# Turning attention probabilities by transposing transfers instead of identity matmuls

## The chip, the cores and the metric

The kernel runs on one core of one Trainium2 chip. The metric is the device time of one execution in microseconds (us), lower is better; the output must agree with the reference. An engine is named as the profile names it: PE is TensorE's matmul stream and PEld its weight loads, DVE is VectorE, ACT is ScalarE, POOL is GpSimd, SP is the engine whose queue issues most transfers.

## The reference

Two layers share a residual stream of 256 tokens by 2048 features, all in float32. The first uses differential attention, the second multi-head latent attention; each then cross-attends into 256 memory tokens and applies a squared-ReLU MLP.

```python
# differential attention, one block of 128 query rows
s = jnp.einsum('bqhcd,bkhcd->bhcqk', qi, k).astype(jnp.float32) * scale
s = jnp.where(causal_mask(q0, S), s, -jnp.inf)
p = jax.nn.softmax(s, axis=-1)
a = (p[:, :, 0] - lam * p[:, :, 1]).astype(v.dtype)
return jnp.einsum('bhqk,bkhd->bqhd', a, v)
...
# latent attention, one block of 128 query rows
s = jnp.einsum('bqhd,bkhd->bhqk', qi, k).astype(jnp.float32) * scale
s = jnp.where(causal_mask(q0, S), s, -jnp.inf)
p = jax.nn.softmax(s, axis=-1).astype(v.dtype)
return jnp.einsum('bhqk,bkhd->bqhd', p, v)
```

What matters here is the step between the two einsums. The softmax runs along a row, so the scores lie with queries on the partitions; the weighted sum over keys needs the probabilities with keys on the partitions. So each 128x128 block of probabilities has to be turned.

## The kernel before

**Arithmetic.** Every float32 factor of a matmul is split into a high part (a cast to PE's reduced float32, on ACT) and a low part (the difference, on DVE); a product is three matmuls: high by high, high by low, low by high. So every operand that is made on the way, the turned probabilities too, costs one ACT cast and one DVE subtract.

**Weights.** They stream from HBM in units of 128 x 2048 words (1 MB) into a pool of seven `raw` buffers (`RAWS`), are split in halves of 1024 columns into `whi` and `wlo` (L221, L222; four buffers each), and are used by PE for 24 matmuls of 512 columns. `take` hands out the next unit and `fill` loads and splits ahead, four units (`AHEAD`). All these loads are issued by SP (`load`, L189) and kept in program order.

**The order.** PE's order is written out by the program itself: the dense work (projections, MLP) runs in a line, and side work is put between by a small planner. A `Task` is a generator that yields a number of us, by a clock that counts PE's planned time, after which its next piece is emitted (`pump`). The constants are `T_SM` 6.5, `T_EV` 2.6, `T_TURN` 2.6, `T_LAND` 7.0 and others. The orders of ACT, DVE and POOL are made by a scheduler from the dependencies. Up to four PSUM banks serve side tasks (`side_bank`, `give_back`).

**Attention.** Both attentions run in four groups of heads. In group gi the attention is started (`attend`), then the projection of the group before it is multiplied (latent; the differential one weaves its projections in later), then the next group's queries, keys and values are made (`project`). So an attention's small steps lie between the dense matmuls of other groups.

- Differential (`attend_diff`): three blocks a group. Each makes scores in a PSUM bank, a softmax, and the difference `a` (128 x 256 words), waits `T_SM + 6.3 + slack`, turns `a` with two flips (`prob_T`), splits it into a `raw` buffer, waits `T_TURN + 1.6`, and multiplies by the values.
- Latent and cross (`attend4`): two head pairs p and two row tiles t give four blocks a group. Each makes scores, a softmax and the normalised `p` (128 x 256 words for t = 0 under the causal mask, else 128 x 512), waits `T_SM + slack`, turns it with two or four flips, and splits it into `pTs`, two `raw` buffers that the group holds until its weighted sum. The weighted sum (`weighted`) starts once all four blocks are done.

A flip (L174) is a matmul by the identity, which puts a turned 128x128 block into PSUM.

**Transposing transfers already in use.** Activations in other places are turned by the DMA rings: `half_words` copies a tile on ACT into two planes of 16-bit halves (low and high halves of each float32, L377), POOL stores them to DRAM (`turned`, L379), SP issues a transposing transfer back into SBUF (`turned_by_dma`, L384, 16-bit elements), and the landed halves lie so that they read as float32 again. 66 tiles take this way, in the projections of the differential attention and in the MLP.

**Buffers.** `p`, `planes`, `landed`, `xg`, `os`, `ks` and the rows and tiles of the rotary embedding all come from one ring of seven SBUF tiles of 128 x 512 words (tag `ev`, `EVS = 7`).

Of the kernel before, what the change touches and what calls it, by code (L numbers as in the profile page):

```python
# [10 lines left out]
F32 = mybir.dt.float32  # L11
F32R = mybir.dt.float32r
I32 = mybir.dt.int32
U16 = mybir.dt.uint16
# [4 lines left out]
P = 128  # L19
# [3 lines left out]
CH = 512  # L23
# [7 lines left out]
EVS = 7  # L31
# [21 lines left out]
def trunk(ctx, tc, x, xT, xT0, mem, memT, positions, gcols, gfinal, lam_vecs, consts, W, out):  # L53
    nc = tc.nc
# [9 lines left out]
    work = pool("work", 2)  # L64
# [6 lines left out]
    def nm(s):  # L71
        serial[0] += 1
        return f"{s}_{serial[0]}"
# [88 lines left out]
    def give_back():  # L162
        free_banks[0] += 1
# [8 lines left out]
    def flip(o, src):  # L172
        clock[0] += 0.109
        nc.tensor.transpose(o, src, ident)  # L174
# [207 lines left out]
    def turned_by_dma(there):  # L382
        landed = work.tile([P, 4, 2 * P], U16, tag="ev", name=nm("landed"), bufs=EVS)
        tc.keep_in_program_order(nc.sync.dma_start_transpose(landed, there))  # L384
        return landed.bitcast(F32).rearrange("p k t -> p k t")

    def split_landed(dst, t, src):
        at = slice(t * P, (t + 1) * P)
        hi = dst[:, 0, :, at]
        tc.keep_in_program_order(nc.scalar.copy(hi, src))  # L390
        nc.vector.tensor_tensor(dst[:, 1, :, at], src, f32(hi), ALU.subtract)  # L391
# [234 lines left out]

    def prob_T(src, n, pt):

        for i in range(n):
            flip(pt[:, i * P : (i + 1) * P], src[:, i * P : (i + 1) * P])  # L630
        o = raw_tile().bitcast(F32R)[:, : 2 * CH].rearrange("p (a c) -> p a c", a=2)
        nc.scalar.copy(o[:, 0, : n * P], pt[:, : n * P])
        nc.vector.tensor_tensor(o[:, 1, : n * P], pt[:, : n * P], f32(o[:, 0, : n * P]), ALU.subtract)
        return o
# [21 lines left out]
    def masks(n):  # L656
        return mask.unsqueeze(1).broadcast_to([P, n, P])

    def attend4(score_pairs, inputs, v, dst, causal, scales=(1.0, 1.0), slack=0.0):


        pTs = [raw_tile().bitcast(F32R).rearrange("p (a b c d) -> p a b c d", a=2, b=2, c=2) for _ in range(2)]

        def probs(t, p, nk):


            sb = yield from side_bank()
            heads = (2 * p, 2 * p + 1)
            pr = work.tile([P, CH], F32, tag="ev", name=nm("p"), bufs=EVS)[:, : 2 * nk]
            rows = pr.rearrange("p (h k) -> p h k", k=nk)  # L670
            if nk == P:
                view = sb.rearrange("p (h a k) -> p h a k", h=2, a=2)
                scores(view, [score_pairs(h, True) for h in heads], t, False)
                nc.vector.tensor_tensor(rows, view[:, :, 1], masks(2), ALU.add)
                nc.vector.tensor_tensor(rows, rows, view[:, :, 0], ALU.add)
                pr, rs = softmax(pr, 2, pr, scales[t])
            else:
                scores(sb.rearrange("p (h k) -> p h k", k=nk), [score_pairs(h, False) for h in heads], t, causal)
                pr, rs = softmax(sb, 2, pr, scales[t])
            nc.vector.tensor_tensor(rows, rows, rs[:, :2].unsqueeze(2).broadcast_to([P, 2, nk]), ALU.mult)  # L680
            yield T_SM + slack
            nb = nk // P
            for i in range(2 * nb):
                flip(sb[:, i * P : (i + 1) * P], pr[:, i * P : (i + 1) * P])
            src = sb[:, : 2 * nk].rearrange("p (h b q) -> p h b q", h=2, b=nb)
            hi = pTs[p][:, 0, :, :nb, t * P : (t + 1) * P]
            nc.scalar.copy(hi, src)
            nc.vector.tensor_tensor(pTs[p][:, 1, :, :nb, t * P : (t + 1) * P], src, f32(hi), ALU.subtract)
            give_back()
            yield T_TURN  # L690

        def weighted(po, p, i, kb, passes, first, last):
            vt = v() if callable(v) else v
            q = slice(kb * P if causal else 0, S)
            o = po[:, i * S : (i + 1) * S][:, q]
            for j, (sv, sp) in enumerate(passes):
                mmul(
                    o, val(vt, sv, kb, (2 * p + i) * P, P), pTs[p][:, sp, i, kb, q],
                    first and j == 0, last and j == len(passes) - 1,
                )  # L700

        def result(p, po):
            hi = dst[:, 0, 2 * p : 2 * p + 2, :]
            src = po.rearrange("p (h q) -> p h q", h=2)
            with urgent():
                nc.scalar.copy(hi, src)
                nc.vector.tensor_tensor(dst[:, 1, 2 * p : 2 * p + 2, :], src, f32(hi), ALU.subtract)

        PASSES = ((0, 0), (0, 1), (1, 0))

        def task():
            for i in inputs:
                yield i
            blocks = []
            for p in range(2):
                for t in range(NT):
                    blocks.append(Task(probs(t, p, P if causal and t == 0 else S)))
                    yield 1.3
            for b in blocks:
                yield b  # L720
            if causal:
                for p in range(2):
                    po = yield from side_bank()
                    for i in range(2):
                        for kb in range(2):
                            weighted(po, p, i, kb, PASSES, kb == 0, kb == 1)
                    result(p, po)
                    give_back()
                    yield 1.3
            else:  # L730
                pos_ = []
                for p in range(2):
                    pos_.append((yield from side_bank()))
                while not v():
                    yield 0.5
                for p in range(2):
                    for i in range(2):
                        weighted(pos_[p], p, i, 0, PASSES, i == 0, False)
                for p in range(2):
                    for passes in (PASSES[:2], PASSES[2:]):  # L740
                        for i in range(2):
                            weighted(pos_[p], p, i, 1, passes, False, passes == PASSES[2:] and i == 1)
                    result(p, pos_[p])
                    give_back()
            yield T_TURN

        dst.run(task())

    def attend_diff(q, k, v, dst, coef, subcols, slack=0.0):


        def block(t, heads, out):
            nk = (t + 1) * P
            sb = yield from side_bank()
            comps = [s for h in heads for s in (2 * h, 2 * h + 1)]
            scores(sb.rearrange("p (c k) -> p c k", k=nk), [whole(q, k, s, nk) for s in comps], t, True)
            n = 2 * len(heads)
            with urgent():
                pr, rs = softmax(sb, n)
                nc.vector.tensor_tensor(rs[:, :n], rs[:, :n], coef[:, :n], ALU.mult)  # L760
                a = work.tile([P, S], F32, tag="a", name=nm("a"))
                for i in range(len(heads)):
                    p0 = pr[:, 2 * i * nk : (2 * i + 1) * nk]
                    p1 = pr[:, (2 * i + 1) * nk : (2 * i + 2) * nk]
                    ai = a[:, i * nk : (i + 1) * nk]
                    nc.vector.tensor_scalar(ai, p1, rs[:, 2 * i + 1 : 2 * i + 2], None, ALU.mult)
                    nc.vector.scalar_tensor_tensor(ai, p0, rs[:, 2 * i : 2 * i + 1], ai, ALU.mult, ALU.add)
            yield T_SM + 6.3 + slack
            pT = prob_T(a, 2, sb)
            give_back()  # L770
            yield T_TURN + 1.6
            if not out:
                out.append((yield from side_bank()))
            po = out[0]
            nb = nk // P
            for i, h in enumerate(heads):
                for kb in range(nb):
                    blk = slice((i * nb + kb) * P, (i * nb + kb + 1) * P)
                    mm3(
                        po[:, h * S : (h + 1) * S], pT[:, 0, blk], pT[:, 1, blk],  # L780
                        val(v, 0, kb, h * S, S), val(v, 1, kb, h * S, S), kb == 0, kb == nb - 1,
                    )
# [792 lines left out]
    def project_diff(gi):  # L1575
# [14 lines left out]
    da_slacks = [0.0, 0.0, 2.0, 1.2]  # L1590
    norm, m, mk = attention(
        project_diff,
        lambda h, o: attend_diff(*h, o, coef, gsub, da_slacks.pop(0)),
        lambda gi: mem_norm() if gi == 1 else None,
        G_CROSS, da_pairs,
    )
# [150 lines left out]
    def attend_latent(held, o):  # L1747
        qr, q, k, v = held
        attend4(
            lambda h, first: side_by_side(q, k, h) + [(qr[:, h], (krope[:, :, :P],))]  # L1750
            if first
            else whole(q, k, h, S) + [(qr[:, h], (krope[:, 0], krope[:, 1]))],
            qr.tasks + q.tasks + k.tasks + krope.tasks, v, o, True, rq, slacks.pop(0),
        )

    norm, m, mk = attention(project_latent, attend_latent, sooner, G_CROSS + 16)
# [150 lines left out]
```

## Time and profile before

| | |
|---|---|
| median of three runs | 2170.72 us |
| range of the runs | 2170.44 to 2171.89 us |
| span of the profiled execution, first to last instruction (the profile has no other time for it) | 2169.0 us |
| granted PE clock, mean | 0.999 |
| differential attention with its projections | about 0 to 390 us |
| latent attention with its projections | about 1150 to 1410 us |
| matmuls of PE, recorded | 10187 |
| moved by the DMA rings | 543.89 MB, mean 251 GB/s |

How it is read: busy time of an engine is the union of its instructions' durations. PE's matmuls are pipelined, so their durations overlap and the distance between starts is what one costs. A list of waits names, for an engine and line, what ended an idle time before it, with the total, the number of times and the longest. A row of a group gives line, engine, operation, out<-in, shapes and count, and then shortest, median and longest duration in ns or the busy time and mean. A `q` after an engine means its sequencer or its queue.

### The profile page before, as it was taken

How to read it: one execution, taken by the hardware profiler on the slowest of the kernel's cores; microseconds unless marked ns; L12 is line 12 of the kernel's file. 1: busy time of each engine (PE TensorE's matmuls, PEld its weight loads, DVE VectorE, ACT ScalarE, POOL GpSimd, SP SyncE). 2: the span in 40 equal slices, each digit the busy share in tenths (PEclk: the TensorE clock that was granted, in tenths of full speed). 3: DMA queues.
4: the chain of work that ended last, by engine and by line, in shares of the span. 5: the costliest groups of instructions: out<-in, count | busy, mean ns of one | idle time of the engine just before them, and what ended most of it. 6: DMA issues, size and time to landing. Idle time of an engine off the chain costs nothing.

```text
span 2169.0 us, 27519 instructions
## 1 busy us (share of the span) xinstructions
PE 2155.4 (99%) x10187; PEld 1805.5 (83%) x10187; DVE 1740.2 (80%) x1962; ACT 1465.6 (68%) x1938; POOL 221.0 (10%) x336
## 2 busy tenths in 40 slices
PE   9999999999999999999999999999999999999998
PEld 7888888888888888888889988888888888888887
DVE  6656878788788889788886878778888888888887
ACT  7556756666767777776665755666777778677665
POOL 1113210001000000000000420000000000000001
PEclk9999999999999999999999999999999999999999
DMA  9477896548989999998986344645998999999895
GB/s 386 151 248 234 260 293 222 194 151 267 297 280 267 308 282 256 319 274 260 306 251 218 103 170 155 221 168 182 283 299 292 258 317 280 266 285 310 254 315 149
DMA packets 151863, 543.89 MB, mean 251 GB/s; under 512 B 79536, under 2 KB 79920, under 8 KB 92848
## 3 DMA queue, kind: packets, MB, share of 16 engines
q1 hardware_dynamic: 134496, 440.14, 56.9%
q0 software_dynamic: 16800, 101.20, 22.5%
q8 instruction: 80, 1.31, 0.2%
q10 hardware_dynamic: 432, 0.79, 0.1%
q14 instruction: 55, 0.45, 0.1%
HBM read 505.38 MB, written 19.40 MB: 242 GB/s over the span
## 4 chain that ended last, share of the span: by engine, by line
PE 95%; DVE 3%; DMA 1%; issue 1%; ACT 0%; DVEq 0%; POOLq 0%; POOL 0%
PE mm L170 62%; PE pr L170 28%; PE ax L170 3%; DVE wlo L222 1%; DMA raw<-in_mlp_wup_dram 1%; PE ax L174 1%; PE mm L174 1%; DVE raw L887 0%; DVE unit L391 0%; ACT whi L221 0%; DVE x L545 0%; DMA raw<-in_da_wqkv_dram 0%; PE pr L174 0%; DVE p L680 0%; DVE ev L1722 0%
## 5 line engine op out<-in xcount | busy, mean ns | idle before, releaser
L222 DVE TENSOR_TENSOR wlo<-raw,whi 128x1024 fp32r<-128x1024 f32 (+3 forms) x946 | 1138.8, 1217 | 335.5 <-ACT whi L221 313.7
L221 ACT CAST whi<-raw 128x1024 fp32r<-128x1024 f32 (+2 forms) x945 | 985.3, 1045 | 576.8 <-PE mm L170 420.0
L170 PE MATMUL mm<-whi,unit 128*128 128x512 f32 (+2 forms) x4000 | 1271.2, 389 | 1.3 <-DVE unit L391 0.9
L170 PEld LDWEIGHTS mm<-whi,unit 128*128 128x128 f32 x4000 | 749.1, 188 | 149.6 <-DVE unit L391 1.7
L170 PE MATMUL mm<-wlo,unit 128*128 128x512 f32 (+2 forms) x2000 | 774.1, 387 | 0.2
L170 PE MATMUL pr<-whi,unit 128*128 128x512 f32 x1912 | 610.5, 389 | 0.0
L170 PEld LDWEIGHTS mm<-wlo,unit 128*128 128x128 f32 x2000 | 376.2, 188 | 72.8 <-DVE wlo L222 3.0
L170 PEld LDWEIGHTS pr<-whi,unit 128*128 128x128 f32 x1912 | 358.8, 188 | 73.4
L170 PE MATMUL pr<-wlo,unit 128*128 128x512 f32 x956 | 372.3, 389 | 1.5 <-DVE wlo L222 1.5
L170 PEld LDWEIGHTS pr<-wlo,unit 128*128 128x128 f32 x956 | 179.7, 188 | 40.0 <-DVE wlo L222 3.6
L379 POOL DMA_DIRECT2D turned<-planes x66 | 37.7, 572 | 673.5 <-ACT planes L377 661.2
L887 DVE TENSOR_TENSOR raw<-raw,raw 128x2048 f32<-128x2048 f32 x40 | 91.5, 2288 | 8.8 <-DMA raw<-in_mlp_wup_dram 8.6
L545 DVE TENSOR_TENSOR x<-x,mm 128x512 f32<-128x512 f32 x128 | 85.3, 682 | 14.1 <-PE mm L170 14.0
L879 POOL DMA_DIRECT2D raw<-in_mlp_wup_dram x48 | 43.4, 905 | 447.8 <-DVE wlo L222 445.2
L431 POOL TENSOR_TENSOR rs<-rs,mhalf 128x1 f32<-128x1 f32 (+1 forms) x26 | 24.9, 962 | 408.1 <-DVE rs L430 408.0
L222 DVE TENSOR_TENSOR wlo<-unit,whi 128x1024 fp32r<-128x1024 f32 x48 | 57.3, 1221 | 5.2 <-ACT whi L221 4.0
L221 ACT CAST whi<-unit 128x1024 fp32r<-128x1024 f32 x48 | 49.8, 1053 | 9.7 <-PE pr L170 9.7
L377 ACT COPY planes<-p 128x1024 uint16<-128x1024 uint16 x48 | 50.0, 1041 | 0.3
L170 PE MATMUL mm<-unit,whi 128*128 128x256 f32 x256 | 46.9, 285 | 0.0
L425 ACT ACTIVATE junk<-x 128x512 bf16<-128x512 f32 (+1 forms) x57 | 35.3, 620 | 10.1 <-DVE x L1092 5.0
L1457 ACT ACTIVATE p<-p,r 128x512 f32<-128x512 f32 x42 | 30.4, 724 | 16.4 <-DVE p L962 7.4
L170 PEld LDWEIGHTS mm<-unit,whi 128*128 128x128 f32 x256 | 40.2, 192 | 0.3
(199 smaller groups left out, 1280.7 us busy)
## 6 DMA issues: line engine op xcount, KB each, us to landing
raw<-in_mlp_wdown_dram SPq DMA_DIRECT2D x128, 1024.0 KB, 7.3
raw<-in_mlp_wup_dram SPq DMA_DIRECT2D x120, 1024.0 KB, 6.9
raw<-in_mlp_wup_dram POOLq DMA_DIRECT2D x48, 1024.0 KB, 9.1
raw<-in_da_wqkv_dram SPq DMA_DIRECT2D x45, 1024.0 KB, 9.8
turned<-planes POOLq DMA_DIRECT2D x66, 256.0 KB, 6.4
raw<-in_da_wo_dram SPq DMA_DIRECT2D x16, 1024.0 KB, 7.0
raw<-in_ca_wkv_dram SPq DMA_DIRECT2D x16, 1024.0 KB, 6.7
raw<-in_mlp_wdown_dram POOLq DMA_DIRECT2D x16, 1024.0 KB, 10.7
```

The source lines that it names most:

```text
L170: return nc.tensor.matmul(o, stationary, moving, start=start, stop=stop, skip_group_check=onto)
L174: nc.tensor.transpose(o, src, ident)
L221: nc.scalar.copy(hi, r)
L222: nc.vector.tensor_tensor(lo, r, f32(hi), ALU.subtract)
L377: nc.scalar.copy(planes, src.bitcast(U16).rearrange("p (w s) -> p s w", s=2))
L379: nc.gpsimd.dma_start(there.rearrange("(q s) w -> q s w", s=2), planes)
L425: return nc.scalar.activation(junk[:, : src.shape[1]], src, AF.Square, scale=scale, accum_out=acc)
L431: nc.gpsimd.tensor_tensor(r[:, :n], r[:, :n], mhalf.broadcast_to([P, n]), ALU.pow)
L545: nc.vector.tensor_tensor(xc, xc, ps, ALU.add)
L879: tc.keep_in_program_order(nc.gpsimd.dma_start(onto, src, accum_op=ALU.add))
L887: nc.vector.tensor_tensor(o, o, q, ALU.add)
L1457: nc.scalar.activation(r, src, AF.Relu, scale=rstd[t])
```

## The change

In the differential attention's groups 0 to 2 and the latent attention's groups 1 to 3 (`sent`), the flips are replaced. ACT copies the probabilities into two 16-bit planes in SBUF (`planes_of`); SP issues one transposing transfer that reads the planes from SBUF and writes the turned planes to SBUF (`turned_planes`), with no store to DRAM and no POOL work; ACT joins the two landed planes into float32 words (`words_of`). The split into high and low part then reads these words from SBUF in place of PSUM. The PSUM bank of the scores is given back before the transfer is issued, and the planner's waits become `T_SM`, `T_EV`, `T_LAND`, `T_TURN + 1.0` in the latent attention, and the old wait, `T_LAND`, `T_TURN + 1.6` in the differential one. The three new tiles of a block come from the `ev` ring. The other groups and the cross attention stay as they were.

```diff
+    def planes_of(src):
+        n = src.shape[1]
+        planes = work.tile([P, 2 * n], U16, tag="ev", name=nm("planes"), padded_shape=[P, 2 * CH], bufs=EVS)
+        nc.scalar.copy(planes.rearrange("p (s w) -> p s w", s=2), src.bitcast(U16).rearrange("p (w s) -> p s w", s=2))
+        return planes
+
+    def turned_planes(planes):
+        n = planes.shape[1] // P
+        landed = work.tile([P, n * P], U16, tag="ev", name=nm("landed"), padded_shape=[P, 2 * CH], bufs=EVS).rearrange("p (n t) -> p n t", t=P)
+        tc.keep_in_program_order(nc.sync.dma_start_transpose(landed, planes))
+        return landed
+
+    def words_of(landed):
+        n = landed.shape[1] // 2
+        words = work.tile([P, n * P], F32, tag="ev", name=nm("words"), padded_shape=[P, CH], bufs=EVS).rearrange("p (n t) -> p n t", t=P)
+        nc.scalar.copy(words.bitcast(U16).rearrange("p k (t s) -> p s k t", s=2), landed.rearrange("p (s k) t -> p s k t", s=2))
+        return words
...
     def prob_T(src, n, pt):
 
-        for i in range(n):
-            flip(pt[:, i * P : (i + 1) * P], src[:, i * P : (i + 1) * P])
+        if pt is not None:
+            for i in range(n):
+                flip(pt[:, i * P : (i + 1) * P], src[:, i * P : (i + 1) * P])
+        else:
+            pt = src.rearrange("p k t -> p (k t)")
...
-            yield T_SM + slack
             nb = nk // P
-            for i in range(2 * nb):
-                flip(sb[:, i * P : (i + 1) * P], pr[:, i * P : (i + 1) * P])
-            src = sb[:, : 2 * nk].rearrange("p (h b q) -> p h b q", h=2, b=nb)
+            if sent:
+                planes = planes_of(pr)
+                yield T_SM
+                give_back()
+                yield T_EV
+                landed = turned_planes(planes)
+                yield T_LAND
+                src = words_of(landed).rearrange("p (h b) q -> p h b q", h=2)
+            else:
+                yield T_SM + slack
+                for i in range(2 * nb):
+                    flip(sb[:, i * P : (i + 1) * P], pr[:, i * P : (i + 1) * P])
+                src = sb[:, : 2 * nk].rearrange("p (h b q) -> p h b q", h=2, b=nb)
...
-            give_back()
-            yield T_TURN
+            if not sent:
+                give_back()
+            yield T_TURN + (1.0 if sent else 0.0)
...
+                planes = planes_of(a) if sent else None
             yield T_SM + 6.3 + slack
-            pT = prob_T(a, 2, sb)
-            give_back()
+            if sent:
+                give_back()
+                landed = turned_planes(planes)
+                yield T_LAND
+                pT = prob_T(words_of(landed), 2, None)
+            else:
+                pT = prob_T(a, 2, sb)
+                give_back()
             yield T_TURN + 1.6
...
-        lambda h, o: attend_diff(*h, o, coef, gsub, da_slacks.pop(0)),
+        lambda h, o: attend_diff(*h, o, coef, gsub, da_slacks.pop(0), bool(da_slacks)),
...
-            qr.tasks + q.tasks + k.tasks + krope.tasks, v, o, True, rq, slacks.pop(0),
+            qr.tasks + q.tasks + k.tasks + krope.tasks, v, o, True, rq, slacks.pop(0), len(slacks) < 3,
```

More of the change, by code (lines that the diff above doesn't have):

```diff
@@ L657, in masks, with attend4 @@
         return mask.unsqueeze(1).broadcast_to([P, n, P])
-    def attend4(score_pairs, inputs, v, dst, causal, scales=(1.0, 1.0), slack=0.0):
+    def attend4(score_pairs, inputs, v, dst, causal, scales=(1.0, 1.0), slack=0.0, sent=False):
         pTs = [raw_tile().bitcast(F32R).rearrange("p (a b c d) -> p a b c d", a=2, b=2, c=2) for _ in range(2)]
@@ L747, in attend4, with attend_diff @@
         dst.run(task())
-    def attend_diff(q, k, v, dst, coef, subcols, slack=0.0):
+    def attend_diff(q, k, v, dst, coef, subcols, slack=0.0, sent=False):
         def block(t, heads, out):
```

## The prediction, made before the changed kernel was run

> **What bounds the kernel now.** I read the page first, then PE's waits, then PE's timeline around the transposes by identity.
>
> ```profile
> span 2169.0 us, 27519 instructions
> PE 2155.4 (99%) x10187; PEld 1805.5 (83%) x10187; DVE 1740.2 (80%) x1962; ACT 1465.6 (68%) x1938; POOL 221.0 (10%) x336
> PE 95%; DVE 3%; DMA 1%; issue 1%; ACT 0%; DVEq 0%; POOLq 0%; POOL 0%
> ...
> PE pr L170 <- DVE wlo L222: 1.5, 3, 1.1
> ...
> PE mm L170 <- DVE unit L391: 0.9, 2, 0.5
> PE ax L174 <- DVE ev L1722: 0.7, 2, 0.5
> ```
>
> The chain that ended last is PE for 95% of the span, and PE's list of waits holds only a few us in all. So PE's instruction stream is the time: what leaves it is saved, and every new wait in it is paid in full. One of the few waits (0.7 us in two places) is at a transpose in the latent attention, where rotary rows are late.
>
> What a removed transpose is worth is read from starts, since a matmul's own duration overlaps its neighbour's:
>
> ```profile
> 1314.77 0.39 PE L170 MATMUL mm<-whi,unit 128*128 128x512 f32 x1
> 1315.01 0.60 PE L174 MATMUL ax<-identr,p 128*128 128x128 f32 x4
> 1315.36 0.47 PE L170 MATMUL mm<-whi,unit 128*128 128x512 f32 x1
> 1315.67 0.40 PE L170 MATMUL mm<-wlo,unit 128*128 128x512 f32 x1
> 1315.91 0.63 PE L170 MATMUL mm<-whi,unit 128*128 128x512 f32 x2
> ...
> 105.96 5.46 PE mm L170 x24
> ...
> L174 PE MATMUL ax<-identr,p x112: 270/272/274, 440.7 to 2079.7; 128*128 128x128 f32 x112
> L174 PE MATMUL ax<-identr,a x24: 270/272/274, 95.5 to 355.8; 128*128 128x128 f32 x24
> ```
>
> From 1314.77 to 1315.91 lie three 512-wide matmuls and four transposes, 1.14 us. 24 such matmuls in a row, one weight unit's, take 5.46 (0.2275 each). So four transposes cost 1.14 - 0.68 = 0.46, or 0.116 us each. The 272 ns of the last two rows are latency, not the price.
>
> **The change part by part.**
>
> *Removed.* `attend_diff` calls `prob_T` for three blocks a group with two flips each (the 24 of `a` are four groups of six); groups 0 to 2 are sent, so 18 go. `attend4` makes 2 + 4 flips for each of two head pairs, 12 a group; latent groups 1 to 3 are sent (`len(slacks) < 3` is read after the pop), so 36 go. Cross attention keeps its own. 54 x 0.116 = **6.3 us** off PE.
>
> *Added on ScalarE.* Per block one copy into two 16-bit planes and one copy that joins the landed planes to words.
>
> ```profile
> L377 ACT COPY planes<-p x48: 1037/1041/1047, 552.3 to 1993.5; 128x1024 uint16<-128x1024 uint16 x48
> ...
> L390 ACT CAST unit<-landed x52: 610/617/626, 546.0 to 2039.3; 128x512 fp32r<-128x512 f32 x52
> ...
> ACT whi L221 <- PE mm L170: 420.0, 347, 2.7
> ```
>
> A block of 512 words is 1024 halves, 1.04 us a copy; one of 256 words is 512 halves, which no row shows as a copy: 0.62 us by the nearest row of 512 elements, between 0.5 (half of 1041) and 1.04. Differential: 9 blocks x 2 x 0.62 = 11.2 us. Latent, a group: 4 x 1.04 + 4 x 0.62 = 6.6; three groups 19.9. Together 31 us on an engine busy 68%. Its usual idle time is spent waiting for PE to free a weight half (420 us in 347 waits), so it runs ahead of PE and I cost these copies at nothing; without that cover all 31 us would fall on PE. VectorE gets no new instruction; its subtracts and ScalarE's casts only move some 7 to 8 us later, and read SBUF in place of PSUM.
>
> The tightest stretches are two latent ones:
>
> ```profile
> 1250.00:1272.00 22.00, 21.54 (x120) 18.34 (x119) 19.66 (x39) 14.41 (x34) 13.79 (x24) 1.00 0.26 89
> ...
> 1345.00:1375.00 30.00, 30.00 (x166) 25.80 (x166) 28.72 (x56) 20.41 (x44) 0.00 (x0) 1.00 0.47 160
> ...
> L687 ACT CAST raw<-ax x4: 367/478/587, 1261.2 to 1270.0; 128x256 fp32r<-128x256 f32 x2, 128x512 fp32r<-128x512 f32 x2
> L688 DVE TENSOR_TENSOR raw<-ax,raw x4: 410/552/687, 1263.9 to 1271.1; 128x256 fp32r<-128x256 f32 x2, 128x512 fp32r<-128x512 f32 x2
> ```
>
> (In the first two the busy times are PE, weight loads, VectorE, ScalarE, POOL; the last but one number is the DMA rings' share. The others are the casts and subtracts that follow the flips of group 1.) In 1250 to 1272, group 1, VectorE is busy 89%, in 1345 to 1375, group 3, 96%. There the four subtracts of a group (two of 0.41, two of 0.69, 2.2 us) leave for later, emptier time: a relief of VectorE, against 3.3 us of plane copies on ScalarE, which has room (14.4 of 22, 20.4 of 30).
>
> *Added on SP and the DMA rings.* 21 transposing transfers, 9 + 12.
>
> ```profile
> L384 SPq DMA_TRANSPOSE landed<-turned x66: 1227/1634/9474, 115.1 to 2014.3; - x66
> ...
> DMA to landing us min/median/max: 3.1/6.0/14.0
> ...
> SPq L189 <- DVE wlo L222: 1403.0, 296, 16.3
> SPq L189 <- PE ax L170: 32.0, 13, 4.8
> ```
>
> None before reads SBUF; the 66 read DRAM, 256 KB each, where the new ones move 128 or 256 KB and need no store beforehand. SP's hold: 1.2 to 9.5 us, taken at the median 1.6, 34 us in all. SP spends 1403 us waiting for buffers, so issuing hides. What queues behind a transfer is the next weight loads, in program order four units of 5.4 us ahead of their use; a wait of SP for the planes delays them by no more than the plan already allows. Landing: 3.1 to 14.0, taken at 6.0.
>
> *Moved.* The plan's constants put the weighted sum later. Latent: before 6.5 + 2.5 + 2.6 = 11.6 us after a block's scores, now 6.5 + 2.6 + 7.0 + 3.6 = 19.7, 8.1 later; differential 7.0 later. PE has other work in that time:
>
> ```profile
> 1257.42 0.52 PE L170 MATMUL ax<-unit,unit 128*128 128x256 f32 x3
> ...
> 1269.34 0.60 PE L174 MATMUL ax<-identr,p 128*128 128x128 f32 x4
> 1272.52 1.49 PE L170 MATMUL ax<-raw,unit 128*128 128x256 f32 x12
> ...
> 1301.31 0.40 PE L170 MATMUL ax<-unit,unit 128*128 128x256 f32 x2
> ...
> 1370.07 0.80 SPq L189 DMA_DIRECT2D raw<-in_memT_dram  x2
> 1371.82 6.56 SPq L189 DMA_DIRECT2D raw<-in_mla_wo_dram  x4
> ...
> 1376.34 1.68 DVE L420 SCALAR_TENSOR_TENSOR unit<-raw,g,unit 128x256 fp32r<-128x256 f32 x4 [1.76 <-ACT unit L416]
> ...
> 1372.80 34.07 PE mm L170 x150
> ```
>
> Group 1's weighted sum goes from 1272.5 to some 1280; its output is wanted by the projection after 1301.3: hidden, and the differential groups have longer. But `pTs` holds two of the seven `raw` buffers until then, and loads wait for that release (SP behind PE L170, 13 times). In group 3 the last memory load (1370.07) would slip to 1378, its halves, done at 1378.0, to 1386; the memory keys start at 1372.8 and reach their fourth unit 3 x 5.46 later, at 1389.2. Hidden with 3 us to spare: the thinnest cover.
>
> PSUM banks come back when the planes are copied, before the transpose, so nothing waits longer for a bank. SBUF does: planes, landed and words all come from the seven `ev` buffers.
>
> *New waits of PE.* Not shown before. Below: -0.7, if relief of VectorE removes the rotary wait quoted above. Above: 10, from the slow rival. I take 1.2, about the longest single wait in PE's list above (1.1), once, in group 1, where the same seven buffers serve the rotary tiles.
>
> *Sum.* 2169.0 - 6.3 + 1.2 = 2163.9 of span. The median of the three runs, 2170.7, is 1.7 above this profile's span (what lies around it), so **2165.6**.
>
> **The rivals.**
>
> *Landing late (little left).* For the largest block the plan leaves 7.0 + 3.6 = 10.6 us from issue to the weighted sum. Landing 6.0, join 1.04, cast 0.62 and subtract 0.69 make 8.4: 2.2 spare. Each us of landing beyond 8.2 stalls PE once in each latent group; the differential blocks (11.2 against 6.0 + 0.62 + 0.37 + 0.42) have 3.8 spare. For it: landings up to 14.0, loads of 1 MB on the same rings, and an SP that reaches its transfer late. Against: DMA is busy only 26 to 47% in the two stretches above. At a landing of 9.5, between median and longest, 1.3 x 3 = 3.9 us of stalls: 2170.7 - 6.3 + 3.9 = 2168.3, within 0.2%. The Trainium skill, VectorE: DVE Perf Modes, The three transpose paths, gives 390 ns for TensorE and 1309 ns for the DMA crossbar on a 128x128 bf16 block, and its rules send such a block to TensorE where PSUM will do. By that price eight such blocks, one after another, would take 10.5 us (an estimate), 2.3 too late for each latent group, and the sum would be 2171.3; the 66 transfers of the same size, landing at 6.0, do not bear it out.
>
> *The ring of seven (slower).* Where the four blocks of group 1 and its rotary tiles meet:
>
> ```profile
> 1250.64 0.40 PE L170 MATMUL ax<-unit,unit 128*128 128x256 f32 x2
> ...
> 1252.74 0.52 PE L170 MATMUL ax<-unit,unit 128*128 128x256 f32 x3
> ...
> 1255.32 0.40 PE L170 MATMUL ax<-unit,unit 128*128 128x256 f32 x2
> ...
> L1721 ACT CAST ev<-ev x4: 397/409/415, 1265.6 to 1268.2; 128x256 fp32r<-128x256 f32 x4
> ```
>
> Scores of group 1's blocks start at 1250.64, 1252.74, 1255.32 and 1257.42, 2.3 us apart, and a transfer takes 6.0: with planes and landed both held, four planes and three landed are seven buffers, before any `p`, word or rotary tile. In group 1 the two rows and up to four rotary tiles (written 1265.6 to 1268.2) lie in the same ring. If a transfer must wait for the one before to land, the fourth lands 9.1 + 4 x 6.0 = 33.1 us after the first scores, against a plan of 6.8 + 9.1 + 7.0 = 22.9: 10.2 late. In that one group alone: 2170.7 - 6.3 + 10.2 = 2174.6, slower; in all three far more. It decides once fewer than some five buffers are left to four blocks. Against: landings can be as short as 3.1, and groups 2 and 3 have no rotary tiles.
>
> That the change does not do what it says I give nothing: the flips stand in a branch that is left. A transfer from SBUF that is far slower than one from DRAM would show as the first rival, or as the second.
>
> **How the numbers follow.** Forecast 0.50; late landing 0.32; the ring or a slow transfer 0.18. About 0.2% (4.3 us) is what a measurement of this kernel can tell from no change, so faster means under 2166.4. Of the forecast 0.06 fall over that line, of the late landing 0.07 under it, of the ring 0.02 stay within 0.2%: faster 0.50 - 0.06 + 0.07 = 0.51, same 0.06 + 0.25 + 0.02 = 0.33, slower 0.16. The range runs from 2163.4 (all flips, the old wait gone, 2170.7 - 6.3 - 0.7 = 2163.7, and a little) to 2174.6; the likeliest case alone is 2163.4 to 2167.
>
> **What would show it.** Right: 54 fewer identity matmuls on `a` and `p`; 21 new DMA_TRANSPOSE with landings under 8 us; no PE wait over 1 us at the weighted sums; weight loads landing as before. Wrong: PE waiting for the low half of `pTs` (late landing); SP or ScalarE waiting for an `ev` tile, or PE for rotary rows by several us (ring); PE waiting at the fourth unit of the memory keys (`raw`).

## The result and the profile after

The changed kernel takes 2205.23 us (median of four runs, 2204.02 to 2206.09) beside 2171.3 us for the kernel before (median of four): a ratio of 1.0155, 95% interval 1.0143 to 1.0167. It is 34 us slower; 2165.6 was predicted, and the range ended at 2174.6. Of the runs in this document one is left out, of the kernel before, beside E17 and E18: it was slow, 2502.9 us at a granted clock of 0.81.

The page of the changed kernel, header, busy times and the chain that ended last:

```profile
span 2202.3 us, 27490 instructions
PE 2159.8 (98%) x10133; PEld 1805.1 (82%) x10133; DVE 1741.7 (79%) x1962; ACT 1497.4 (68%) x1980; POOL 215.3 (10%) x336
PE 91%; DVE 3%; DMA 2%; ACT 2%; issue 1%; POOL 0%; SPq 0%; DVEq 0%; POOLq 0%; ACTq 0%
```

PE has the 54 matmuls fewer (10187 to 10133), ScalarE 31.8 us more. PE's share of the chain fell from 95% to 91%: other work now ends PE's waits. Its list of waits (engine line <- what ended the wait: total us, times, longest us):

```profile
PE ax L174 <- DVE ev L1760: 10.3, 3, 9.1
PE ax L170 <- ACT raw L717: 6.6, 2, 6.4
PE ax L170 <- ACT raw L653: 4.9, 2, 2.5
PE mm L170 <- DVE wlo L222: 3.8, 2, 2.2
PE mm L170 <- DVE unit L409: 2.8, 2, 2.4
PE ax L170 <- DVE raw L718: 1.9, 2, 1.0
```

These six lines hold 30.3 us, where the same list of before held a few. Taken over the whole trace, the distance from each matmul's start to the next, less the plan's own price of it (columns / 2400 + 0.0133 us, at least 0.109), adds up to 16.3 us before and 54.9 after: 38.6 more. Less the 5.9 of 54 flips at that price this is 32.7 of the 33.3 us by which the span grew (2169.0 to 2202.3). So the flips were saved, and more than six times as much was lost in waits and in stretches at half clock behind them, at four places: 228 to 270 us (differential group 2), 1284 (latent group 1), 1357 (group 2) and 1406 (group 3).

The greatest is in latent group 1. SP's timeline there (start, duration, what):

```profile
1255.21 0.42 SPq L189 DMA_DIRECT2D raw<-in_mla_ukv_dram  x1
1280.98 11.06 SPq L396 DMA_TRANSPOSE landed<-planes  x3
1292.10 0.57 SPq L189 DMA_DIRECT2D raw<-in_mla_ukv_dram  x1
1293.28 1.24 SPq L396 DMA_TRANSPOSE landed<-planes  x1
```

ScalarE's timeline in the same stretch, with the idle time before an instruction and what ended it in brackets:

```profile
1266.80 0.62 ACT L390 COPY planes<-p 128x512 uint16<-128x512 uint16 x1
...
1279.88 1.04 ACT L390 COPY planes<-p 128x1024 uint16<-128x1024 uint16 x1 [1.01 <-DVE p L701]
1283.55 0.40 ACT L1759 CAST ev<-ev 128x256 fp32r<-128x256 f32 x1 [2.62 <-DMA landed<-planes]
```

The first block's planes are made at 1267.4, yet its transfer is issued at 1280.98, just as the fourth block's planes copy ends (1279.88 + 1.04) and frees that block's softmax tile. SP's list of waits has it as its longest for a transfer:

```profile
SPq L396 <- ACT planes L390: 69.4, 6, 25.3
```

The tile for the landed planes comes from the ring of seven. By the order of the program the seven at that time were two rotary rows, four planes and the fourth `p`. The rotary cast waits in turn until the first transfer has landed and its planes tile is free. Then PE:

```profile
1284.55 1.09 PE L174 MATMUL ax<-identr,ev 128*128 128x128 f32 x4 [9.05 <-DVE ev L1760]
```

Over 9 us of waiting has a second price. The windows (us, then busy time of PE, weight loads, VectorE, ScalarE, POOL, granted clock, DMA share, GB/s):

```profile
1266.00:1278.80 12.80, 9.50 (x47) 7.71 (x46) 11.85 (x20) 9.25 (x19) 8.03 (x14) 1.00 0.00 0
1278.80:1292.40 13.60, 6.85 (x20) 5.43 (x21) 1.71 (x4) 2.99 (x6) 0.00 (x0) 0.50 0.18 35
1292.40:1300.00 7.60, 7.60 (x35) 6.27 (x34) 3.77 (x5) 3.44 (x5) 0.00 (x0) 1.00 0.96 299
```

The granted clock is 0.50 for 13.6 us, 7.9 of them after PE runs again. In the list of waits the rotary rows stand at 10.3 us; the excess of PE's starts between 1280 and 1300 is 13.7. In group 3 it is the same: a wait of 6.4 us at the weighted sum, then a granted clock of 0.50 from 1405.1 to 1411.8, and 10.1 us of excess in 1400 to 1420.

### The profile page after: what moved, and what is told of

Same layout as the page of the kernel before. It is cut to its first block, busy times and chain, and to the rows that moved or that the text cites. A ratio compares the mean times of both kernels' runs of the same rounds, so it can differ in the third digit from the quotient of the medians.

```text
span 2202.3 us, 27490 instructions
## 1 busy us (share of the span) xinstructions
PE 2159.8 (98%) x10133; PEld 1805.1 (82%) x10133; DVE 1741.7 (79%) x1962; ACT 1497.4 (68%) x1980; POOL 215.3 (10%) x336
## 3 DMA queue, kind: packets, MB, share of 16 engines
q0 software_dynamic: 16800, 101.20, 22.3%
## 4 chain that ended last, share of the span: by engine, by line
PE 91%; DVE 3%; DMA 2%; ACT 2%; issue 1%; POOL 0%; SPq 0%; DVEq 0%; POOLq 0%; ACTq 0%
PE mm L170 59%; PE pr L170 27%; PE ax L170 2%; DVE wlo L222 2%; PE ax L174 1%; DMA raw<-in_mlp_wup_dram 1%; PE mm L174 1%; ACT whi L221 1%; DMA landed<-turned 0%; DMA raw<-in_ca_wkv_dram 0%; DVE unit L409 0%; DMA turned<-planes 0%; DVE x L563 0%; ACT words L402 0%; ACT p L637 0%
```

## The experiments

In the expectations "after" is the changed kernel. Theory A: the ring of seven `ev` tiles, which the new tiles fill. Theory B: the chain from planes to weighted sum is simply longer than planned, or SP's queue is the hindrance. Later: C, ScalarE's in-order work; D, SP standing at transfers while loads wait; E, the `raw` buffers held longer. The times in the table are medians; the ratio and its interval are worked out from the single runs, so the ratio is not exactly the quotient of the two medians.

| run | what is run | us | before | ratio, 95% interval |
|---|---|---|---|---|
| E1 | all sent, few tiles | 2182.92 | 2172.11 | 1.0053 (1.0038 to 1.0068) |
| E2 | differential only | 2184.20 | 2172.11 | 1.0056 (1.0041 to 1.0071) |
| E3 | latent only | 2193.75 | 2172.11 | 1.0103 (1.0086 to 1.0120) |
| E4 | latent group 1 flipped | 2192.26 | 2172.11 | 1.0095 (1.0080 to 1.0110) |
| E5 | flips, both copies | 2187.72 | 2170.83 | 1.0073 (1.0058 to 1.0088) |
| E6 | after, issued by ScalarE | 2217.16 | 2170.83 | 1.0206 (1.0189 to 1.0223) |
| E7 | E1, issued by ScalarE | 2205.66 | 2170.83 | 1.0154 (1.0135 to 1.0172) |
| E8 | E7, latent group 1 flipped | 2195.49 | 2170.83 | 1.0111 (1.0094 to 1.0128) |
| E9 | E1, latent group 1 flipped | 2175.59 | 2171.30 | 1.0020 (1.0011 to 1.0029) |
| E10 | E9, differential group 2 flipped | 2171.40 | 2171.30 | 0.9998 (0.9989 to 1.0007) |
| E11 | E9, differential transfers 8 us later | 2173.64 | 2171.30 | 1.0008 (0.9999 to 1.0017) |
| E12 | latent groups 2 and 3 only, few tiles | 2170.63 | 2171.30 | 0.9997 (0.9988 to 1.0006) |
| E13 | flips, copies behind them | 2173.75 | 2171.16 | 1.0013 (1.0004 to 1.0022) |
| E14 | flips, one copy before them | 2185.07 | 2171.16 | 1.0056 (1.0044 to 1.0069) |
| E15 | flips, unread transfers in differential group 2 | 2172.53 | 2171.16 | 1.0007 (0.9998 to 1.0015) |
| E16 | before, weighted sums later | 2176.43 | 2171.16 | 1.0025 (1.0015 to 1.0034) |
| E17 | E9, split probabilities in the ring | 2184.07 | 2171.99 | 1.0057 (1.0044 to 1.0070) |
| E18 | before, split probabilities in the ring | 2182.84 | 2171.99 | 1.0052 (1.0037 to 1.0066) |

### E1: the same transfers with few tiles

```diff
-                planes = planes_of(pr)
+                planes = planes_of(pr, whole_p[:, CH // 2 :].bitcast(U16) if nk == P else None)
...
-                landed = turned_planes(planes)
+                landed = turned_planes(planes, pr.bitcast(U16))
...
-                src = words_of(landed).rearrange("p (h b) q -> p h b q", h=2)
+                src = words_of(landed, planes).rearrange("p (h b) q -> p h b q", h=2)
...
-                planes = planes_of(a) if sent else None
+                planes = planes_of(a, pr[:, :S].bitcast(U16)) if sent else None
...
-                landed = turned_planes(planes)
+                landed = turned_planes(planes, pr[:, S:].bitcast(U16))
```

> All 21 blocks are still sent, with the same copies, transfers and waits of the plan; only the buffers differ: a block's planes, landed planes and words are put into its own softmax tile and, for the large latent blocks, one more tile, so a latent group takes 6 tiles of the ring of seven in place of 16, and a differential block none beyond its own. Theory A (the ring): the first transfer of latent group 1 is issued within about 3 us of its planes copy in place of 13.5 us after it, the 9.2 us wait of PE for the rotary rows goes with the half clock behind it, and the stalls at 228 to 262 shrink too: 2180 to 2188. Theory B (the chain of copy, transfer, join, cast and subtract is simply longer than the plan allows, or SP's one queue is the hindrance): 2200 to 2206, the stalls stay where they are, late at the weighted sums.

2182.92: 22.3 us of the 34 are gone, with every copy, transfer and planned wait still there. SP's timeline in latent group 1 of E1:

```profile
1261.85 1.19 SPq L397 DMA_TRANSPOSE p<-p  x1
1265.44 1.23 SPq L397 DMA_TRANSPOSE p<-planes  x1
1272.20 1.19 SPq L397 DMA_TRANSPOSE p<-p  x1
```

The first transfer now starts as its own planes copy ends, not as the fourth's does. The 6.4 us at group 3's weighted sum have gone too: PE's list of E1 has no wait for `raw` over 1.3 us. Part of theory A failed: the rotary tiles are still late. A softmax tile is now held until its words are read, which is the likely reason, but no run takes that apart.

```profile
PE ax L174 <- DVE ev L1761: 7.7, 2, 7.5
```

### E2, E3, E4: parts alone

E2 has `False` for `len(slacks) < 3` in the latent call, E3 has it for `bool(da_slacks)` in the differential call, and E4 narrows the latent groups:

```diff
-            ... slacks.pop(0), len(slacks) < 3,
+            ... slacks.pop(0), len(slacks) < 2,
```

> Only the differential blocks are sent (9 transfers), the latent attention keeps its 36 flips. The stalls of after up to 300 us add up to some 11 us (11.0 of excess in 220 to 280), and 18 flips are 2.1 us: theory A and B both expect 2171 + 9 = 2180, if stalls are local to the blocks that are sent. If the latent stalls are set off by something that the differential blocks leave behind, far more.

> Only the latent blocks are sent (12 transfers), the differential attention keeps its 18 flips. Stalls of after in 1280 to 1300 and 1400 to 1420 are 13.7 and 10.1 us, 1.7 at 1340, and 36 flips are 4.2 us: 2171 + 21 = 2192, if stalls are local.

> As after, but latent group 1 keeps its 12 flips (groups 2 and 3 and the differential groups 0 to 2 are sent). Theory A: the 13.7 us at 1280 to 1300 go and 1.4 us of flips come back: 2193. If the wait of the rotary rows were only what is late first, and the time is lost in any case at the next wait behind it: 2203 to 2206.

E2 loses 12.1, E3 21.6, together 33.7 of after's 34: the losses are local, and add. E4 is 13.0 below after, as theory A expected: the time lost at the rotary rows does not come back elsewhere.

### E9, E10, E12: what E1 still loses

E9 puts E4's edit on E1. E10 also has `len(da_slacks) > 1` for `bool(da_slacks)`; E12 has `False` there.

> As E1 (few tiles, transfers issued by SP), but latent group 1 keeps its 12 flips; 42 flips (4.9 us) are saved. Theory A: the 9.2 us that E1 lost at 1260 to 1280 go and 1.4 us of flips come back: 2175, that is +3 beside before. If E1's stall at the rotary rows only moves to the next late tile: 2181 to 2183.

> As E9, and the differential group 2 keeps its 6 flips too: groups 0 and 1 of the differential and 2 and 3 of the latent attention are sent, 36 flips (4.2 us) saved. Theory D says that E1's 6.3 us at 240 to 280 come from SP standing at group 2's first transfer while the stage's loads are held: 2172 - 4.2 + 1 = 2169. If group 2 is not the place, but the sent differential groups together: 2174 or more.

> Only latent groups 2 and 3 are sent, with few tiles, by SP; all other groups keep their flips: 24 flips (2.8 us) saved. In E1 these two groups showed no wait of PE over 1 us. Theories A and D: 2172 - 2.8 = 2169. If ScalarE's 13 us of copies in these groups cost PE something by themselves: 2172 or more.

E9 hits 2175. E10 takes away another 4.2 us with group 2 of the differential attention. Its list of PE's waits is nearly that of before:

```profile
PE mm L170 <- DVE unit L409: 2.1, 2, 1.4
...
PE ax L174 <- DVE ev L1761: 0.7, 2, 0.5
```

But 36 flips less are 4.2 us, and E10 is level with before; E12 with 24 flips less (2.8 us) gains 0.7 by the medians. Both were expected at 2169. By single profiles the spans are 2167.1 and 2167.9 beside 2169.0, 1.9 and 1.1 us less: under half of what the flips are worth. By the sum of starts used above the flips are saved (3.9 and 2.6 us at the plan's price), but the excess is 18.2 and 17.6 beside 16.3. One place is seen: at 1566 us, far behind the last transfer, PE waits for `unit` 1.4 us in E10 and 2.1 in E12, where it waited at most 0.5 before (there L391). E18, which sends nothing, waits 1.4 us at the same place, so this is not shown to come from the transfers. The rest is within what the intervals (2 us each way) leave open.

### E15, E11, E16, E17, E18: differential group 2

E15 keeps all flips and adds planes and transfers that nothing reads, in that group alone (its edit against E1; no other group is sent):

```diff
             if sent:
-                give_back()
                 landed = turned_planes(planes, pr[:, S:].bitcast(U16))
-                yield T_LAND
-                pT = prob_T(words_of(landed, planes), 2, None)
-            else:
-                pT = prob_T(a, 2, sb)
-                give_back()
+            pT = prob_T(a, 2, sb)
+            give_back()
```

> All flips are kept and used. In the differential group 2 alone, planes are made and three transfers are issued by SP as in E1 (into the block's own softmax tile), and nothing reads what lands. Theory D: SP stands at the first of them for some 20 us and the loads behind it come late: 2176 to 2179, with PE waiting for weight halves at 240 to 280 as in E1. If late landing or the join were E1's cause there, nothing waits for a landing here: 2171 to 2173.

E15's SP timeline:

```profile
215.79 1.13 SPq L189 DMA_DIRECT2D raw<-in_da_wo_dram  x1
233.37 1.61 SPq L397 DMA_TRANSPOSE p<-p  x1
235.03 0.78 SPq L189 DMA_DIRECT2D raw<-in_da_wqkv_dram  x1
```

SP stands 16 us at the transfer, and the load behind it, which went at 227 before, goes at 235. PE does not notice: 2172.53, no stall in 240 to 280. Theory D falls for this group: it expected 2176 or more, and E15's interval ends 3.3 us above before. What E15 lacks is the join and the later weighted sum. E16, below, has the later sum alone, and its excess in 240 to 280 is 0.5 beside 0.2 before, so the sum's delay does not explain E9's 5.9. In E9, ScalarE's timeline in the same place:

```profile
241.81 0.61 ACT L391 COPY p<-a 128x512 uint16<-128x512 uint16 x1
242.33 1.04 ACT L221 CAST whi<-raw 128x1024 fp32r<-128x1024 f32 x1
246.93 0.78 ACT L402 COPY p<-p 128x512 uint16<-128x512 uint16 x1 [3.56 <-DMA p<-p]
247.57 1.98 ACT L221 CAST whi<-raw 128x1024 fp32r<-128x1024 f32 x2
249.46 0.40 ACT L653 CAST raw<-p 128x256 fp32r<-128x256 f32 x1
251.71 0.78 ACT L402 COPY p<-p 128x512 uint16<-128x512 uint16 x1 [1.85 <-DMA p<-p]
252.35 1.03 ACT L221 CAST whi<-raw 128x1024 fp32r<-128x1024 f32 x1
```

PE in E9, the matmuls with an idle time before them:

```profile
253.44 0.50 PE L170 MATMUL mm<-whi,unit 128*128 128x512 f32 x1 [0.71 <-ACT whi L221]
...
254.70 0.50 PE L170 MATMUL mm<-wlo,unit 128*128 128x512 f32 x1 [0.76 <-DVE wlo L222]
```

ScalarE stands in its order at the join until the planes have landed, 3.56 and 1.85 us, and the weight casts behind the join are late. A further 1.25 us is the weighted sum itself, which waits at 259.79 for its own low half (DVE raw L654). The landings, E9's transfers at 237.4 and then at 239.3 and 242.4:

```profile
DMA to landing us min/median/max: 2.4/2.4/2.4
...
DMA to landing us min/median/max: 7.6/8.4/9.2
```

As the first goes, the DMA rings' share is 0.02 (235.9 to 237.4); while the others land, beside loads of 1 MB, it is 1.00 (239.3 to 249.0). That fits the stall, but no run takes away the join alone. The other tries:

E11 delays the differential transfers by 8 us of the plan (`yield 8.0` ahead of `turned_planes`).

> As E9, but each differential block issues its transfer 8 us later by the plan, so that two more loads go ahead of it in SP's order; flips saved as in E9. Theory D: the 6.3 us at 240 to 280 go in whole or in half, 2169 to 2172. If they come from ScalarE's copies or from late landing, the later transfer makes it worse: 2176 to 2182.

2173.64: between the theories, its interval overlapping E9's. The excess in 240 to 260 goes (4.7 to under 0.5 us), but 260 to 280 has 4.7 in place of 1.2, and there are 3.8 more at 554. In the profiled run the loss is moved, not removed; by the medians 2.0 us are gained, which the intervals do not tell from nothing.

E16 is before with later weighted sums and nothing else:

```diff
-            yield T_TURN
+            yield T_TURN + (8.1 if sent else 0.0)
...
-            yield T_TURN + 1.6
+            yield T_TURN + 1.6 + (7.0 if sent else 0.0)
```

> Before, with one thing moved: in the groups that the change sends, the weighted sum is planned later, by 8.1 us in the latent and 7.0 us in the differential blocks, and so the two raw buffers of a latent group are held longer. No copies, no transfers. My prediction costed this at nothing: 2170 to 2173. If the held raw buffers delay loads enough to stop PE, above all at the memory keys of latent group 3: 2175 or more.

It costs 5.3 us. In E16's timeline 2.5 us show at one place, two matmuls that wait for weight halves:

```profile
280.50 0.49 PE L170 MATMUL mm<-whi,unit 128*128 128x512 f32 x1 [1.16 <-ACT whi L221]
281.76 0.50 PE L170 MATMUL mm<-wlo,unit 128*128 128x512 f32 x1 [0.77 <-DVE wlo L222]
```

The rest is spread over short waits, most of them in the MLPs, and has no one cause that I can name. The memory keys of latent group 3, the place that I had called thinnest, show none.

E17 and E18 take the differential's split probabilities out of the `raw` buffers:

```diff
-        o = raw_tile().bitcast(F32R)[:, : 2 * CH].rearrange("p (a c) -> p a c", a=2)
+        o = work.tile([P, 2, S], F32R, tag="ev", name=nm("pT"), bufs=EVS)
```

> As E9, with one buffer elsewhere: the split probabilities of a differential block lie in a tile of the ev ring in place of one of the seven raw buffers, which they held in E9 until the later weighted sum (SP there stood from 248.6 to 256.9 for such a release). Theory E (what is left of E9 at 240 to 280 is the raw buffers held longer, so loads come late): those 6 us go, 2168 to 2171. If it is SP standing at the transfer or late landing after all: 2174 to 2177.

> The control for E17: before, with all its flips, and the split probabilities of the differential blocks in the ev ring in place of a raw buffer. 2170 to 2172, since PE has no wait for weights there before; if it gains as much as E17, then E17's gain is not that of the transfers.

Both lose, E18 10.9 us on the kernel before itself: one ring tile more for a differential block, with a `raw` buffer given back for it, is no bargain. So E17 can't settle theory E: its loss in 240 to 280 is as in E9 (6.4 us of excess, 5.9 there), but E18, without transfers, loses 5.6 there too. Whether E18's 10.9 come from the ring or from loads that run further ahead wasn't tried.

### E5, E13, E14: ScalarE's copies, with all flips kept

The copies are of a block's halves onto themselves:

```diff
+    def touch(src):
+        halves = src.bitcast(U16).rearrange("p (w s) -> p s w", s=2)
+        nc.scalar.copy(halves, halves)
```

> All flips are kept and nothing is sent; ScalarE only runs 42 more copies, two for each of the same 21 blocks: each copies the block's 16-bit halves onto themselves, once after the softmax and once after the flips (31 us of ScalarE). My prediction costed these copies at nothing: 2171 to 2174 beside 2172 of before. Theory C (ScalarE's in-order work is what is late): if ScalarE were the cause of the rest that E1 left, 2180.

> As E5 (all flips kept, 42 more ScalarE copies of 16-bit halves onto themselves, 31 us), but both copies of a block stand behind its flips, where no flip waits for them. If E5's 17 us came from the copy that stood between softmax and flips (the chain up to PE has no slack in the latent groups): 2171 to 2174. If they came from ScalarE's time as such: 2184 or more.

> The other half of E5: all flips kept, one copy of halves for each of the 21 blocks, between softmax and flips, none behind the flips (15.5 us of ScalarE). By the chain: nearly all of E5's loss, 2182 to 2188. By ScalarE's time as such: half of it, 2179.

The copies are dearer than the 31 us expected: 0.78 us for 512 halves and 1.37 for 1024, 40 us in all in E5 and E13 and 20 in E14. E5 loses 16.9 us. The same 40 us of copies where no flip waits for them cost 2.6 us (E13). Half of them, between softmax and flips, cost 12 to 14 (E14: 12.2 by the ratio, 13.9 by the medians), and E14's list of PE's waits says where the largest part is:

```profile
PE ax L174 <- ACT p L395: 6.0, 4, 3.5
```

The longest, 3.5 us, is far longer than the copy it waits for (0.77): in ScalarE's order the copy stands behind other work. So the chain from softmax to turning has no slack in the latent groups. In the changed kernel no flip stands there, and the same lateness goes into the transfer's start, so E14's cost doesn't carry over to it as such.

### E6, E7, E8: issued by ScalarE

```diff
-        tc.keep_in_program_order(nc.sync.dma_start_transpose(landed, planes))
+        nc.scalar.dma_start_transpose(landed, planes)
```

> As after, with its four ring tiles for a block, but the 21 transfers are issued by ScalarE, which makes the planes, in place of SP: no weight load stands behind a transfer that waits. Theory A (the ring alone): the transfers still wait for landed tiles, the 9 us stall at the rotary rows stays, and ScalarE itself, which now waits in its order for a tile, may stop the weight casts: 2200 or more. Theory D (SP's one queue blocked by waiting transfers is the main cause): 2180 or less.

> As E1 (two tiles for a block at most), with the transfers issued by ScalarE in place of SP. In E1 SP stood at a transfer from 215.4 to 237.5 while weight loads behind it could have gone at 227, and PE lost 6.3 us in 240 to 280. Theory D says that these are the price of SP's order: they go, the 7.7 us at the rotary rows stay, 2176 to 2178. If the rest of E1 comes from late landing or from ScalarE's copies, no gain, or a loss by ScalarE's issuing (21 x 1.2 = 25 us more on it): 2183 or more.

> As E7, but latent group 1, whose rotary tiles share the ring, keeps its 12 flips; 42 flips (4.9 us) are saved. Theories A and D together: all large stalls are gone, 2172 - 4.9 + 1 = 2168. If a third cause is left: 2173 or more.

All three are worse by 12 to 23 us than the same kernel with SP (after, E1, E9). E8's ScalarE timeline in latent group 3:

```profile
1385.40 2.07 ACTq L397 DMA_TRANSPOSE p<-p  x1
1387.57 1.05 ACT L221 CAST whi<-raw 128x1024 fp32r<-128x1024 f32 x1 [1.25 <-DMA raw<-in_memT_dram]
1393.04 0.76 ACT L402 COPY p<-p 128x512 uint16<-128x512 uint16 x1 [4.42 <-DMA p<-p]
1393.67 1.03 ACT L391 COPY planes<-p 128x1024 uint16<-128x1024 uint16 x1
...
1394.73 1.25 ACTq L397 DMA_TRANSPOSE p<-planes  x1
```

No load stands behind a transfer on SP now. The third transfer's join starts 7.6 us after its issue (1385.4 to 1393.0), ScalarE stands 4.4 us at its join, and the fourth block's planes are queued behind that join. So the fourth transfer leaves at 1394.7, and PE waits 10.6 us at the weighted sum. The Trainium skill, DMA: Bandwidth & Descriptors, Issuing engines are not separate DMA queues, says that transfers share the same DMA engines whoever issues them, and that another issuer saves only the time of issuing. These runs agree: nothing was won, and 12 us and more were lost. In the lists of waits of E8 and E7 two places hold most of it: the weighted sum of group 3 (10.6 and 11.2 us) and a weight half that ScalarE casts late (5.9 and 7.2). E8's timeline shows ScalarE's order behind the first; for the others it is the likely cause.

## Why the prediction was wrong

- **Flips, 6.3 us.** Right in count, and the price holds in the trace of before: at 33 places where two or four flips stand among 512-wide matmuls without a wait, the starts give 0.116 us a flip in twos and 0.113 in fours. What arrives once the large waits are gone is less (E10, E12).
- **ScalarE's copies at nothing.** The 31 us came out at 35.1 by durations: the join costs 0.77 us for 512 halves and 1.36 for 1024, where 0.62 and 1.04 were taken, and the plane copies what was taken. ScalarE's busy time grew by 31.8, since neighbouring instructions overlap a little.

```profile
L402 ACT COPY words<-landed x21: 745/775/1369, 99.8 to 1406.6; 128x512 uint16<-128x512 uint16 x15, 128x1024 uint16<-128x1024 uint16 x6
```

  "Runs ahead of PE" was an average over the span. E13 confirms it nearly, where no flip waits (2.6 us lost for 40 us of copies); E14 shows that it fails between softmax and turning.
- **SP.** Right: 1.2 us a transfer (1.6 taken), and 16 us of standing in front of loads cost nothing that E15 can tell (1.4 us by the medians, interval -0.4 to 3.3).
- **Landing, 6.0 (3.1 to 14.0).** E1's median landings, in the list of DMA issues (the first group 128 KB each, the second 256 KB):

```profile
p<-p SPq DMA_TRANSPOSE x15, 2.4
p<-planes SPq DMA_TRANSPOSE x6, 3.1
```

  Beside loads they were 7.6 and 9.2 (E9). The Trainium skill's 1309 ns for a 128x128 block (VectorE: DVE Perf Modes, The three transpose paths), taken in the prediction as 10.5 us for eight blocks in a row, doesn't hold here as a price for each block: a transfer of eight landed in 3.1. The rival of late landing looked at PE's weighted sum and its 3.8 us to spare in the differential groups; what it did not look at is ScalarE's own order, where E9's trace has most of the loss, at the join (read from the trace, not tested alone).
- **Moved, hidden.** Failed: E16 costs 5.3 us, not at the memory keys; 2.5 of them are two waits for weight halves at 280, the rest is spread.
- **SBUF and the new waits of PE, "1.2, once, in group 1".** This is the step that failed most. The mechanism was among the rivals, with its place, at 0.18: the ring of seven, the rotary tiles. Two things were missed. I counted tiles held at the same time and let the first transfers go; in fact the first landed tile had to wait for the fourth block, so that not one transfer started before 1281. And I took the ring to bind in latent group 1 alone and ended the range there, though the text itself said "in all three far more". E1 shows that tiles cost 22.3 us over all groups, and E9 8.7 more at the rotary rows (7.3 by the two medians and 1.4 of flips). Nor was there a term for the clock, which these waits drop to 0.50.

By the medians the 34 us go in three steps: 22.3 with the tiles that E1 does without, 7.3 with latent group 1 (E9) and 4.2 with differential group 2 (E10). The last two steps also give back flips (1.4 and 0.7), so 8.7 and 4.9 us were lost there. E10 is then level with before, where its flips should have put it 4.2 below. That the first two are tiles and the group with the rotary rows is shown; that the third is ScalarE standing at the join is read from the trace; where the last 4.2 went is open, but for about 1 us at the wait for `unit`. No version beat the kernel before by more than can be measured.

## What to carry to other kernels

Before work is moved from a busy engine to an idle path, write down in order which buffers the new path takes and whose release each waits for: in a ring, the first user can wait for the last. A copy is free only where nothing is waiting behind it, in its data or in its engine's order; test it by adding the copy alone, once on the chain and once off it. A transfer that lands fast in a quiet stretch (here 2.4 us) can land late beside bulk loads (7.6 to 9.2), and an engine that takes its work in order then stands at whatever reads it.

## What was not expected of the hardware

A long wait of PE costs more than itself. The clock fell to 0.50 some 3.3 us into the 9 us wait and stayed there for 13.6 us. The Trainium skill, TensorE: Matmul & The Clock Gate, Part 1: The HAM clock gate, states half rate after an idle window of about 3.4 us, and this wait agrees. Others in these traces do not fit that length. In differential group 2 of the changed kernel PE's last matmul starts at 259.17 and lasts 0.39, the next starts at 262.03 after a wait of 2.48 us, and the clock falls about 2 us into it:

```profile
252.00:261.60 9.60, 6.68 (x30) 5.20 (x30) 6.35 (x9) 7.95 (x15) 2.01 (x3) 1.00 1.00 209
261.60:265.00 3.40, 2.97 (x10) 2.68 (x11) 1.17 (x3) 0.68 (x3) 3.32 (x10) 0.50 0.96 347
```

In E14 PE waits 3.53 us, until 1370.83, at a granted 1.00, and the clock is 0.50 from 1371.4 to 1374.7, when PE is busy again. So the half clock can come before a wait is 3.4 us old, and also behind its end. The waits of E9, 1.25 us at most around 250 to 260, left the clock at 1.00.

The other surprise is how quickly a transposing transfer from SBUF to SBUF lands when the rings are quiet, 2.4 us from issue with nothing else queued.
